# Two more gate pairs start their products ahead of the second half's norm, and TensorE multiplies a constant at the start

## The chip, the cores and the metric

One core of a Trainium2 chip runs the whole block. The metric is the device time of one execution in microseconds. In the names below PE is TensorE (the matrix engine), DVE is VectorE, ACT is ScalarE and SP is SyncE, whose queue issues nearly all DMAs. PEclk is the clock that TensorE was granted as a share of full speed: 1.00 is 2.4 GHz and 0.50 is 1.2 GHz.

## What is computed

One layer of an encoder block, in float32, on 16 meta tokens and 1024 positions of 1024 channels. Only the first part matters here:

```python
h = rmsnorm(h_res, g_mix_pre[l])
proj = h @ w_in[l]
u_a, c_g, b_g, v_b, gate_logits = jnp.split(proj, splits, axis=-1)

y_a = fourier_mix(u_a) @ w_fourier[l]

conv_in = c_g * v_b
y_b = (b_g * centred_dwconv(conv_in, conv_w_mix[l], conv_b_mix[l])) @ w_conv_out[l]

gates = jax.nn.sigmoid((gate_logits + b_gates[l]).reshape(bn, L, N_BRANCHES, D_MODEL))
merged = gates[:, :, 0] * y_a + gates[:, :, 1] * y_b
...
```

Behind it come the output projection, a second norm, a gated MLP with a depthwise convolution, and a last norm.

## The kernel before

**Numbers and products.** Activations lie with channels on partitions and positions along the row; two position halves of 514 columns each (`NH`) are worked on. A float32 operand is split into a high part (a rounding cast, L121, on ScalarE) and a low part (source minus high part, L122, on VectorE). A product is three matmuls per 128 channels: high by high (L153), low activation (L155), low weight (L157), each over two column parts of 258 and 256. `split` is the helper that records L121 and L122.

**Pairs.** Two blocks of 128 output channels and the two position halves are computed together by seven products instead of eight (Strassen-Winograd). `Pair.step` holds them. One product has 4 blocks of 128 channels, so 4 x 3 x 2 = 24 matmuls. Step 0 multiplies by the activation piece `b11` and step 4 by `b21`; both pieces come from the first position half alone. Steps 1, 2, 3, 5 and 6 use `t1`, `t2`, `t3`, `b22` and `t4`, which need the second half too. Step 5 adds to the PSUM tile `d` that step 1 began, and it may do so only when `g_s` (the sum of d and u, L138, in step 2) has read that tile.

**The first 100 us.** The kernel loads the positions' first half (`x1`) and the second (`x2`). One gate pair, (1,0), is computed naturally, without the pair scheme, in `natural`: for the first half while the loads come, with the norm applied to the result, and for the second half (natural(1)) while that half is normalised. Squares of the columns are summed on ScalarE and VectorE, a matmul with the constant `ones` makes the means (`ms_a`, `ms_b`, L433), and `rsqrt_of` makes the reciprocal root (r_a_y, r_a_t, r). `norm` (L438) scales by it on VectorE. Then VectorE makes low parts and the sums and differences of the two halves (L141).

Three gates are "early": `GATES[:NE1]` with `NE1 = 3`, that is (1,1), (1,2) and (1,3), which the trace names g_1, g_2 and g_3. Their weights for steps 0 and 4 are loaded and split by `early_pieces` (g_1e_0, g_1e_1 and so on), and the loop `for i in range(0, NE1, 2)` (L492) does those two steps, two gates at a time, before natural(1) begins in the code. The trace and the order name a gate by its last number only, so that g_0 and g_1 can also mean (0,0) and (0,1), and g_0 with nat the pair (1,0).

**Weights.** `Ring` has seven pieces (a high and a low tile each) and three raw buffers for loads. Four of the seven hold `wn`, the weights of the natural products, until natural(1) is done. Three circulate among the early gates until then.

**The jobs.** `run_pairs` (L320) then goes through 13 jobs: 7 gates and 6 pairs for the convolution branch (C, V, B twice). An early gate takes only steps `LATER` = (1, 2, 3, 5, 6); the others take all seven. While one job computes, the pieces of the next are made and the loads of the one behind that start. Hooks hang work for the Fourier branch on places (job, step): `transformed(kt)` (four matmuls on `wp`, L596, a load and a store) on step 3, and `fold(kt)` (vector work on a load, a store) on step 5 of jobs 3 to 10; `next_fold` loads the first folded blocks (`u`, L635) in the last job.

**What sets the order.** A scheduler places the instructions of each engine from the code's order and their dependences; `behind` and `issue_after` set lower bounds. What it made of the code is the order that each engine follows, and each engine runs its own list in order, SyncE's DMA queue included.

Of the kernel before, what the change touches and what calls it, by code (L numbers as in the profile page):

```python
# [17 lines left out]
P = 128  # L18
D = 1024
KT = D // P  # L20
# [61 lines left out]
def block_kernel(ctx, tc, xT, w_u, w_in, w_fa, w_fa2, w_fb, w_fb2, w_co, w_out, w_up, w_dn,  # L82
                 par, dch, cos_t, sin_t, outT):
    nc = tc.nc
# [21 lines left out]
    ones = const.tile([P, P], F32, name="ones")  # L106
# [3 lines left out]
    warm = const.tile([P, 1], F32, name="warm")  # L110
# [4 lines left out]
    def col(name, i=0, p=P):  # L115
        return pr[:p, _C[name] + i : _C[name] + i + 1]
# [20 lines left out]
    def add(out, a, b, eng=V):  # L137
        return eng.tensor_tensor(out=out, in0=a, in1=b, op=ALU.add).ins  # L138

    def sub(out, a, b, eng=V):  # L140
        eng.tensor_tensor(out=out, in0=a, in1=b, op=ALU.subtract)  # L141
# [124 lines left out]
    class Pair:  # L266


        us = 2
# [46 lines left out]
    def early_pieces(name, src, into=(None, None), eng=V):  # L316

        return ring.halves(f"{name}e", src, into, eng)
# [46 lines left out]
    ring.open(proj_s, "ring1", 7)  # L365
    gp = new_pool(keep_s, "gp", side="right")
    W1 = T0 + NH
    NE1 = 3
    GATES = [(1, 1), (1, 2), (1, 3), (0, 0), (0, 1), (0, 2), (0, 3)]

    class Gate(Pair):
        us = NE1 + 1

        def __init__(self, g, f):
            self.rows = (g * KT + f, g * KT + f + 4)
# [11 lines left out]
    with ExitStack() as st:  # L387
# [36 lines left out]
        def ms_tile(name):  # L424
            return psum.tile([P, 512], F32, tag="ms", name=name, bufs=2)

        ms_a = [ms_tile(f"ms1_a{i}") for i in range(2)]

        def half_norm(name, sums, n, out):
# [10 lines left out]
        def natural(half, kt, x, js=range(2)):  # L440
            for j in js:
                mm3(
                    subs(nat_out[half, j]),
                    tuple(a[:, kt % 4 * P : (kt % 4 + 1) * P] for a in wn[j][kt // 4]),
                    tuple([a[:, kt % 4, o : o + n] for o, n in SUB] for a in x),
                    kt == 0,
                    kt == KT - 1,
                )
# [12 lines left out]
        for kt in range(KT):  # L461
            if kt in (0, 3):
                for j in range(2):
                    i = kt // 3
# [4 lines left out]
                half_norm("a", next(sa), W1, r1[:, :W1])  # L469
            natural(0, kt, raw1[kt // 4])  # L470
        early = [Gate(*g) for g in GATES[:NE1]]
        ep = [early_pieces(p_.name, w_in[16 + p_.rows[0]]) for p_ in early]
        first = []

        def x_b(k):
            if k == 1:
                for j in range(2):
                    s = scratch["t3"][0][:, j, :]
                    mul(s, whole(nat_out[0, j]), r1[:, T0:W1])
                    first.append(s)  # L480
            norm(k, x1[k], r1[:, :W1])
            x1[k] = x1[k][:, T0:]
            put(hx["b11" if k < 4 else "b21"], k % 4, x1[k])
# [6 lines left out]
        for k in range(4, KT):  # L490
            x_b(k)
        for i in range(0, NE1, 2):  # L492
            for step, e in ((0, 0), (4, 1)):
                for p_, w in zip(early[i : i + 2], ep[i : i + 2]):
                    p_.step(psum, step, w[e], hx[PIECES[step]])
# [37 lines left out]
    class Conv(Pair):  # L533


        us = NE1 + 1

        def __init__(self, kind, j, state):
            self.kind, self.j, self.state = kind, j, state
# [40 lines left out]
    jobs = []  # L580
    for p_ in early + [Gate(g, f) for g, f in GATES[NE1:]]:
        jobs.append((p_, [w_in[16 + r] for r in p_.rows], LATER if p_ in early else ALL))
# [7 lines left out]
    def transformed(kt):  # L590

        r = ring.raw(f"wu{kt}")
        SP.dma_start(r[:, :512], w_u[kt])
        wp = wtile(psum, f"wp{kt}")[:, :512]
        for g in range(G):
            nc.tensor.matmul(wp[:, g * P : (g + 1) * P], r[:, g * P : (g + 1) * P], dc, start=True, stop=True)  # L596
        src = wp.rearrange("p (g k) -> p g k", k=P)
        t = r[:, 512:]
        for s, at, k in ((src[:, :, :KC], slice(0, NA), KC), (src[:, :, KC:], slice(NA, 512), KS)):
            S.copy(t[:, at].rearrange("p (g k) -> p g k", k=k), s)  # L600
        SP.dma_start(fold_d[kt, :, FW:], t)

    def fold(kt):

        t = pre.tile([P, 2 * H + HP], F32, tag="fold", name=f"fold{kt}", bufs=1)
        h, diff = t[:, : L + 1], t[:, 2 * H : 3 * H]
        SP.dma_start(h[:, :L], xT[:, kt, :])
        V.scalar_tensor_tensor(out=h[:, :L], in0=h[:, :L], scalar=col("g_pre", kt), in1=r1, op0=ALU.mult, op1=ALU.mult)
        V.tensor_copy(h[:, L : L + 1], h[:, 0:1])
        f0, rev = h[:, :H], h[:, L : L - H : -1]  # L610
        sub(diff, f0, rev)
        add(f0, f0, rev)
        c, s = t[:, H : 2 * H], t[:, :H]
        add(c[:, :Q], f0[:, :Q], f0[:, H - 1 : H - 1 - Q : -1])
        sub(c[:, Q:], f0[:, : Q - 1], f0[:, H - 1 : H - Q : -1])
        sub(s[:, :Q], diff[:, :Q], diff[:, H - 1 : H - 1 - Q : -1])
        add(s[:, Q:], diff[:, 1:Q], diff[:, H - 2 : H - 1 - Q : -1])
        SP.dma_start(fold_d[kt, :, :FW], t[:, :FW])
# [12 lines left out]
    def next_fold(kt):  # L631

        raw, hi, lo = (room(t, dt, f"u{kt}{i}") for i, (t, dt) in enumerate(zip(FOLD_ROOMS[kt], (F32, F32R, F32R))))
        w = FW + 512
        SP.dma_start(raw[:, :w], fold_d[kt])  # L635
        split(hi[:, :w], lo[:, :w], raw[:, :w])
        xs = [(hi[:, at : at + H], lo[:, at : at + H]) for at in (H, 0)]
        folded.append((xs, (hi[:, FW:w], lo[:, FW:w])))

    hooks = {(NE1 + kt, 3): lambda kt=kt: transformed(kt) for kt in range(KT)}  # L640
    for kt in range(KT):
        hooks[NE1 + kt, 5] = lambda kt=kt: fold(kt)
    hooks[len(jobs) - 1, 1] = lambda: next_fold(0)
    hooks[len(jobs) - 1, 2] = lambda: next_fold(1)
    hooks[len(jobs) - 1, 4] = lambda: next_fold(2)
# [64 lines left out]
    with ExitStack() as st:  # L710
# [18 lines left out]
        def table(tab, name, at):  # L729
            raw = room(at, F32, f"{name}r")[:LT, :TW]  # L730
            return raw, SP.dma_start(raw, tab).ins
# [7 lines left out]
        for kt in range(KT):  # L739
# [3 lines left out]
            if kt == 0:  # L743
                cos_r, _ = table(cos_t, "cos", "t4h")
# [143 lines left out]
    def load_merged(c):  # L888
        c0, n = CHM[c]
        v = valid(c)  # L890
        parts = []
        for k in range(0, KT, 3):
            e = min(k + 3, KT)
            t = ring.raw(f"mr{c}_{k}")[:, : (e - k) * n].rearrange("p (k n) -> p k n", n=n)
            SP.dma_start(t[:, :, :v], merged_d[:, k:e, c0 + TM - T0 : c0 + TM - T0 + v])
            if v < n:
                V.memset(t[:, :, v:], 0.0)
            parts += [merged_parts(c, kt, t[:, kt - k])[0] for kt in range(k, e)]
        merged[c] = parts
# [32 lines left out]
    def norm_a(c):  # L932
        c0, n = CHM[c]
        v = valid(c)
        ms = next(z[c])
        rr = np_.tile([P, W], F32, tag="rr", name=f"rr{c}", bufs=2)[:, :n]
        got = rsqrt_of(f"r2_{c}", scratch, ms, n, rr)
        sq = squares(f"h{c}", n)
        next(sq)
        xr = []  # L940
        for f in range(0, KT, 2):
            t = eo.tile([P, 2 * W], F32, tag="o", name=f"xr{c}_{f}", bufs=4)
            t = t.rearrange("p (f n) -> p f n", f=2)
            SP.dma_start(t[:, :, :v], xT[:, f : f + 2, TM + c0 : TM + c0 + v])
            xr += [t[:, i, :v] for i in range(2)]
        for f in range(KT):
            h = h_at(c, f)
            scaled = mul(h, h, rr).ins
            add(h[:, :v], h[:, :v], xr[f])
            sq.send(h)  # L950
            SP.dma_start(hres_d[:, f, c0 : c0 + v], h[:, :v])
        z[c] = sq
        return got, scaled
# [8 lines left out]
    def norm_b(c):  # L962
        c0, n = CHM[c]
        if c not in rs:
            inverse(c)
        rr = rs[c]
        A, B = second(c)
        for f in range(KT):
            h = h_at(c, f)
            V.scalar_tensor_tensor(out=h, in0=h, scalar=col("g_fpre", f), in1=rr, op0=ALU.mult, op1=ALU.mult)  # L970
            if c < 2:
                a, e = max(c0, 1), min(c0 + n, NH + 1)
                put(hx["b11" if f < 4 else "b21"], f % 4, hA[f // 4][:, f % 4, a:e], a - 1, e - a)
            elif f < 4:
                sub(A(f), h, A(f))
                put(hx["t1"], f, A(f), c0 - 513, n)
            else:
                put(hx["b22"], f - 4, B(f), c0 - 513, n)
# [16 lines left out]
    def mean_b(c):  # L995
        z[c] = next(z[c])
# [118 lines left out]
    ep = [None]  # L1115
# [18 lines left out]
    for c in range(1, 4):  # L1134
        hooks = {0: lambda: norm_a(c - 1), 5: lambda: (load_merged(c + 1), mean_b(c - 1), norm_b(c - 1))}
        order = range(KT)
        if c == 3:
            order = (6, 7, 0, 1, 4, 5, 2, 3)
            hooks = {
                0: lambda: norm_a(2),  # L1140
                3: lambda: plain.load(0, "t1h"),
                4: lambda: first_blocks("t3h"),
                5: lambda: (mean_b(2), inverse(2)),
            }
# [7 lines left out]
    early = lambda step, i: ups[i].step(psum, step, ep[i][step // 4], hx["b11" if step == 0 else "b21"])  # L1152
# [309 lines left out]
```

## Time and profile before

| | us |
|---|---|
| median of three runs | 1236.94 |
| the three runs | 1235.50, 1236.94, 1240.91 |
| the profiled execution | 1235.98 |
| its span, first to last instruction | 1234.2 |
| PE busy in the span | 1182.5 |
| DVE busy | 1004.5 |
| ACT busy | 549.3 |
| mean granted clock of PE | 0.985 |

Times within the trace are counted from the span's start. A busy time is what an engine's instructions took; a wait is the idle time ahead of an instruction, with the instruction that ended it. Matmuls overlap, so the distance from one start to the next tells their pace better than their duration does. Where several instructions of one form follow each other, a row of a timeline joins them, with their number as x2, x4 and so on.

### The profile page before, as it was taken

How to read it: one execution, taken by the hardware profiler on the slowest of the kernel's cores; microseconds unless marked ns; L12 is line 12 of the kernel's file. 1: busy time of each engine (PE TensorE's matmuls, PEld its weight loads, DVE VectorE, ACT ScalarE, POOL GpSimd, SP SyncE). 2: the span in 40 equal slices, each digit the busy share in tenths (PEclk: the TensorE clock that was granted, in tenths of full speed). 3: DMA queues.
4: the chain of work that ended last, by engine and by line, in shares of the span. 5: the costliest groups of instructions: out<-in, count | busy, mean ns of one | idle time of the engine just before them, and what ended most of it. 6: DMA issues, size and time to landing. Idle time of an engine off the chain costs nothing.

```text
span 1234.2 us, 22254 instructions
## 1 busy us (share of the span) xinstructions
PE 1182.5 (96%) x8800; PEld 1136.5 (92%) x8800; DVE 1004.5 (81%) x1771; ACT 549.3 (45%) x997; POOL 0.4 (0%) x6
## 2 busy tenths in 40 slices
PE   7979999999999899999989999999999999999995
PEld 6879999999998899898989999999999998888884
DVE  8998757766677766889999988899888989866678
ACT  6733433322352235655644435443444444454562
POOL 0000000000000000000000000000000000000000
PEclk8989999999999999999989999999999999999998
DMA  6245554221786755562233332232223289344433
GB/s 245 87 129 191 173 188 157 98 99 50 252 244 205 242 184 104 133 109 86 86 112 112 112 112 69 95 129 95 89 84 120 96 313 327 127 158 124 130 126 137
DMA packets 75016, 176.65 MB, mean 143 GB/s; under 512 B 7550, under 2 KB 24526, under 8 KB 74912
## 3 DMA queue, kind: packets, MB, share of 16 engines
q1 hardware_dynamic: 74768, 175.11, 44.7%
q8 instruction: 69, 1.13, 0.4%
q14 instruction: 35, 0.29, 0.1%
q10 hardware_dynamic: 144, 0.12, 0.0%
HBM read 126.57 MB, written 48.63 MB: 142 GB/s over the span
## 4 chain that ended last, share of the span: by engine, by line
PE 76%; DVE 14%; DMA 7%; ACT 2%; issue 1%; DVEq 0%; SPq 0%; ACTq 0%
DMA wor<-in_w_out_dram 3%; PE up_d L153 3%; PE up_d L155 3%; PE up_d L157 3%; PE up_a L153 3%; PE up_a L157 3%; PE up_c L157 3%; PE up_c L155 3%; PE up_c L153 3%; PE up_a L155 3%; PE dna L155 3%; PE dna L153 3%; PE dna L157 3%; PE dnb L155 2%; PE dnb L153 2%; PE dnb L157 2%
## 5 line engine op out<-in xcount | busy, mean ns | idle before, releaser
L153 PE MATMUL mo<-mh,wo 128*128 128x258 f32 (+1 forms) x256 | 73.4, 287 | 0.0
L157 PE MATMUL mo<-mh,wo 128*128 128x258 f32 (+1 forms) x256 | 72.4, 283 | 0.0
L155 PE MATMUL mo<-ml,wo 128*128 128x258 f32 (+1 forms) x256 | 72.2, 282 | 0.0
L153 PEld LDWEIGHTS mo<-mh,wo 128*128 128x128 f32 x256 | 48.5, 189 | 0.4 <-ACT hA L926 0.2
L155 PEld LDWEIGHTS mo<-ml,wo 128*128 128x128 f32 x256 | 48.5, 189 | 0.2
L157 PEld LDWEIGHTS mo<-mh,wo 128*128 128x128 f32 x256 | 48.5, 189 | 0.0
L1077 ACT ACTIVATE up_1o<-up_1x,pr 128x512 f32<-128x512 f32 x33 | 27.0, 817 | 42.4 <-DVE up_1x L138 42.4
L1081 ACT ACTIVATE up_0o<-up_0o 128x512 f32<-128x512 f32 x44 | 27.8, 632 | 31.9 <-DVE up_0o L1079 31.7
L121 ACT CAST up_1h<-up_1t 128x512 fp32r<-128x512 f32 x11 | 6.8, 620 | 78.0 <-DVE up_1t L138 78.0
L153 PE MATMUL up_d<-b22h,up_5h 128*128 128x258 f32 (+1 forms) x168 | 34.8, 290 | 6.3 <-DVE up_0x L138 6.1
L138 DVE TENSOR_TENSOR up_u<-up_b,up_u 128x514 f32<-128x514 f32 x21 | 14.6, 695 | 29.0 <-PE up_b L157 28.9
L155 PE MATMUL up_d<-b22l,up_5h 128*128 128x258 f32 (+1 forms) x168 | 34.8, 290 | 0.0
L157 PE MATMUL up_d<-b22h,up_5l 128*128 128x258 f32 (+1 forms) x168 | 34.5, 287 | 0.0
L157 PE MATMUL up_c<-t3h,up_3l 128*128 128x258 f32 (+1 forms) x168 | 33.9, 283 | 0.4 <-DVE up_3l L122 0.4
L157 PE MATMUL up_d<-t1h,up_1l 128*128 128x258 f32 (+1 forms) x168 | 33.6, 281 | 0.5 <-DVE up_1l L122 0.5
L153 PE MATMUL up_d<-t1h,up_1h 128*128 128x258 f32 (+1 forms) x168 | 33.9, 282 | 0.1
L153 PE MATMUL up_b<-t2h,up_2h 128*128 128x258 f32 (+1 forms) x168 | 33.9, 283 | 0.0
L153 PE MATMUL up_c<-t3h,up_3h 128*128 128x258 f32 (+1 forms) x168 | 33.8, 283 | 0.0
L157 PE MATMUL up_c<-t4h,up_6l 128*128 128x258 f32 (+1 forms) x168 | 33.8, 282 | 0.0
L155 PE MATMUL up_c<-t3l,up_3h 128*128 128x258 f32 (+1 forms) x168 | 33.7, 281 | 0.0
L155 PE MATMUL up_c<-t4l,up_6h 128*128 128x258 f32 (+1 forms) x168 | 33.7, 282 | 0.0
L157 PE MATMUL up_b<-t2h,up_2l 128*128 128x258 f32 (+1 forms) x168 | 33.7, 282 | 0.0
(1298 smaller groups left out, 4344.9 us busy)
## 6 DMA issues: line engine op xcount, KB each, us to landing
g<-gp_d SPq DMA_DIRECT2D x35, 512.0 KB
up_1r<-in_w_up_dram SPq DMA_DIRECT2D x22, 512.0 KB
gp_d<-up_0o SPq DMA_DIRECT2D x44, 256.0 KB
up_0r<-in_w_up_dram SPq DMA_DIRECT2D x20, 512.0 KB
s<-sig_d SPq DMA_DIRECT2D x16, 514.0 KB
sig_d<-g_s SPq DMA_DIRECT2D x30, 257.0 KB
u<-fold_d SPq DMA_DIRECT2D x8, 777.0 KB
fold_d<-fold SPq DMA_DIRECT2D x8, 521.0 KB
```

Source lines behind the costliest of these rows:

```text
L121: a = copy(hi, src)
L138: return eng.tensor_tensor(out=out, in0=a, in1=b, op=ALU.add).ins
L153: nc.tensor.matmul(o, wh, h, start=first, stop=False, **kw)
L155: nc.tensor.matmul(o, wh, l, start=False, stop=False, **kw)
L157: newest[:] = [nc.tensor.matmul(o, wl, h, start=False, stop=last, **kw).ins]
L1077: S.activation(t, ap[:, 1 : 1 + HALF], AF.Identity, bias=col("cb_ffn", b), scale=w(1))
L1081: S.activation(t, t, AF.Gelu_apprx_tanh)
```

## The change

The constant `NE1` goes from 3 to 5, so that (0,0) and (0,1) are early too: their steps 0 and 4 come before the jobs, and their jobs keep five steps. The number of `u` tiles, `NE1 + 1` = 4 before, is `NE1` = 5 now. The weights of the first three early gates are loaded where all were; the others' are asked for within the loop. Eleven matmuls of the constant `ones` by itself stand ahead of everything on TensorE, into a PSUM tile of the `ms` kind that is not read. The hooks hang on jobs `NE1 + kt` and so move from jobs 3 to 10 to jobs 5 to 12; the last fold hangs on step 0, since step 5 of the last job has a hook of its own.

```diff
-    NE1 = 3
+    NE1 = 5
...
     class Gate(Pair):
-        us = NE1 + 1
+        us = NE1
...
+        w0 = ms_tile("warm")[:, :P]
+        for _ in range(11):
+            nc.tensor.matmul(w0, ones, ones, start=True, stop=True)
         ms_a = [ms_tile(f"ms1_a{i}") for i in range(2)]
...
         early = [Gate(*g) for g in GATES[:NE1]]
-        ep = [early_pieces(p_.name, w_in[16 + p_.rows[0]]) for p_ in early]
+        first_weights = lambda ps: [early_pieces(p_.name, w_in[16 + p_.rows[0]]) for p_ in ps]
+        ep = first_weights(early[:3])
...
         for i in range(0, NE1, 2):
+            ep += first_weights(early[len(ep) : i + 2])
             for step, e in ((0, 0), (4, 1)):
                 for p_, w in zip(early[i : i + 2], ep[i : i + 2]):
                     p_.step(psum, step, w[e], hx[PIECES[step]])
...
     class Conv(Pair):
-        us = NE1 + 1
+        us = NE1
...
     hooks = {(NE1 + kt, 3): lambda kt=kt: transformed(kt) for kt in range(KT)}
     for kt in range(KT):
-        hooks[NE1 + kt, 5] = lambda kt=kt: fold(kt)
+        hooks[NE1 + kt, 5 if kt < KT - 1 else 0] = lambda kt=kt: fold(kt)
```

How this moves instructions is shown on three engines. First VectorE, where the norm of the second half begins (x_2_118 and its like are columns of the second half, t4 holds high and low parts of it, t3l and x_2_110 are the first half's columns). Before:

```order
L122 TENSOR_TENSOR t4l<-x_1_117,t4h 128x514
L141 TENSOR_TENSOR t3l<-x_1_117,t3l 128x514
L438 SCALAR_TENSOR_TENSOR x_2_118<-x_2_118,pr,r_83 128x514
L438 SCALAR_TENSOR_TENSOR x_3_119<-x_3_119,pr,r_83 128x514
L141 TENSOR_TENSOR x_2_110<-x_2_118,x_2_110 128x514
L122 TENSOR_TENSOR t4l<-x_2_118,t4h 128x514
L122 TENSOR_TENSOR t4l<-x_3_119,t4h 128x514
```

The same place in VectorE's list now:

```order
L122 TENSOR_TENSOR g_0e_0l<-g_0er,g_0e_0h 128x512
L141 TENSOR_TENSOR t3l<-x_1_117,t3l 128x514
L122 TENSOR_TENSOR g_0e_1l<-g_0er,g_0e_1h 128x512
L442 SCALAR_TENSOR_TENSOR x_2_118<-x_2_118,pr,r_83 128x514
L442 SCALAR_TENSOR_TENSOR x_3_119<-x_3_119,pr,r_83 128x514
L141 TENSOR_TENSOR x_2_110<-x_2_118,x_2_110 128x514
L122 TENSOR_TENSOR t4l<-x_2_118,t4h 128x514
L122 TENSOR_TENSOR g_1e_0l<-g_1er,g_1e_0h 128x512
L122 TENSOR_TENSOR t4l<-x_3_119,t4h 128x514
L141 TENSOR_TENSOR x_3_111<-x_3_119,x_3_111 128x514
L442 SCALAR_TENSOR_TENSOR x_4_120<-x_4_120,pr,r_83 128x514
L122 TENSOR_TENSOR g_1e_1l<-g_1er,g_1e_1h 128x512
```

Four low parts of weights (g_0e_0l, g_0e_1l, g_1e_0l, g_1e_1l) stand among the columns of the second half. Second, ScalarE at the same place, before:

```order
L384 ACTIVATE g_1_s_482<-g_1_a,pr 128x514
L384 ACTIVATE g_2_s_509<-g_2_a,pr 128x514
L121 CAST t1h<-t3l 128x514
L284 COPY g_3_u<-g_3_a 128x514
L121 CAST t1h<-t3l 128x514
L121 CAST t4h<-x_2_118 128x514
L121 CAST t4h<-x_3_119 128x514
```

And now:

```order
L384 ACTIVATE g_1_s_494<-g_1_a,pr 128x514
L121 CAST g_0e_0h<-g_0er 128x512
L384 ACTIVATE g_2_s_521<-g_2_a,pr 128x514
L121 CAST g_0e_1h<-g_0er 128x512
L284 COPY g_3_u<-g_3_a 128x514
L121 CAST t1h<-t3l 128x514 x2
L121 CAST t4h<-x_2_118 128x514
L121 CAST g_1e_0h<-g_1er 128x512
L284 COPY g_0_u<-g_0_a 128x514
L121 CAST t4h<-x_3_119 128x514
```

The casts of the new pieces stand between sigmoids of earlier gates and casts of t4. Third, TensorE behind step 0 of g_3, before:

```order
L157 MATMUL g_3_a<-b11h,g_3e_0l 128x256
L153 MATMUL nat_0_566<-t4h,wn_0h 128x258
L153 MATMUL nat_0_566<-t4h,wn_0h 128x256
L155 MATMUL nat_0_566<-t4l,wn_0h 128x258
L155 MATMUL nat_0_566<-t4l,wn_0h 128x256
L157 MATMUL nat_0_566<-t4h,wn_0l 128x258
L157 MATMUL nat_0_566<-t4h,wn_0l 128x256
L153 MATMUL g_3_a<-b21h,g_3e_1h 128x258
```

And now:

```order
L157 MATMUL g_3_a<-b11h,g_3e_0l 128x256
L153 MATMUL g_0_a<-b11h,g_0e_0h 128x258
L153 MATMUL g_0_a<-b11h,g_0e_0h 128x256
L155 MATMUL g_0_a<-b11l,g_0e_0h 128x258
L155 MATMUL g_0_a<-b11l,g_0e_0h 128x256
L157 MATMUL g_0_a<-b11h,g_0e_0l 128x258
L157 MATMUL g_0_a<-b11h,g_0e_0l 128x256
```

Step 0 of g_0 follows step 0 of g_3, then come step 4 of both and step 0 of the second g_1; natural(1) begins behind that, and step 4 of this g_1 stands behind its first six matmuls.

## Rows read from the trace of the kernel before

**Rows 1.** Busy time by stretch: PE, PEld, DVE, ACT, POOL; PEclk; DMA share.

```profile
core 0: us, PE busy (x) PEld busy (x) DVE busy (x) ACT busy (x) POOL busy (x), PEclk, DMA share, GB/s
...
45.00:59.80 14.80, 14.80 (x122) 14.49 (x121) 14.80 (x25) 9.44 (x17) 0.00 (x0) 1.00 0.28 89
59.80:62.70 2.90, 0.13 (x2) 0.04 (x1) 2.90 (x6) 2.90 (x7) 0.00 (x0) 1.00 0.48 182
62.70:74.10 11.40, 9.63 (x71) 8.82 (x72) 11.40 (x20) 4.58 (x8) 0.00 (x0) 1.00 0.31 98
74.10:78.10 4.00, 0.30 (x4) 0.12 (x2) 3.98 (x10) 0.62 (x1) 0.00 (x0) 0.66 0.46 133
78.10:82.10 4.00, 4.00 (x19) 4.00 (x20) 4.00 (x8) 1.34 (x2) 0.00 (x0) 0.50 0.17 66
82.10:88.00 5.90, 5.90 (x50) 5.90 (x50) 5.32 (x12) 3.69 (x6) 0.00 (x0) 0.99 0.25 64
```

**Rows 2.** Waits of PE, 0 to 330 us: us in total, times, longest.

```profile
PE nat L153 <- DVE wn_0h L121: 6.4, 1, 6.4
PE g_d L153 <- DVE g_s L138: 3.7, 1, 3.7
PE g_d L153 <- ACT g_1h L121: 2.8, 1, 2.8
...
PE g_a L153 <- ACT g_3e_0h L121: 0.5, 1, 0.5
```

**Rows 3.** Chain of waits, ahead of step 5: start, us, what.

```profile
74.20 1.91 DVE t4l L122 x4
...
77.26 0.70 DVE g_s L138
```

**Rows 4.** Timeline of PE: steps 5 and 6 of job 0; steps 0 and 1 of job 12.

```profile
78.09 0.77 PE L153 MATMUL g_d<-b22h,g_5h 128*128 128x258 f32 x2 [3.70 <-DVE g_s L138]
...
82.85 0.41 PE L153 MATMUL g_c<-t4h,g_6h 128*128 128x258 f32 x2
...
302.66 0.40 PE L153 MATMUL B_a<-b11h,B_0h 128*128 128x258 f32 x2
...
305.54 0.41 PE L153 MATMUL B_d<-t1h,B_1h 128*128 128x258 f32 x2
```

**Rows 5.** Timeline of DVE: a weight's low part and the row behind it.

```profile
43.53 0.69 DVE L122 TENSOR_TENSOR g_3e_1l<-g_3er,g_3e_1h 128x512 fp32r<-128x512 f32 x1
44.14 0.69 DVE L122 TENSOR_TENSOR t4l<-x,t4h 128x514 fp32r<-128x514 f32 x1
```

**Rows 6.** Waits of ACT, 15 to 80 us: those of weight casts.

```profile
ACT g_3e_0h L121 <- ACT g_2e_1h L121: 1.0, 1, 1.0
...
ACT g_3e_1h L121 <- PE g_a L155: 0.6, 1, 0.6
```

**Rows 7.** Chain of waits, 100 to 140 us: products of wp.

```profile
126.11 0.89 PE wp L596 x8
```

**Rows 8.** Chain of waits: first, ninth and tenth pair of nat's matmuls.

```profile
6.35 0.77 PE nat L153 x2
...
10.14 0.43 PE nat L157 x2
10.57 0.26 PE nat L153 x2
```

**Rows 9.** Timeline of DVE where the first half's mean comes back.

```profile
19.10 0.70 DVE L138 TENSOR_TENSOR sq_b<-sq_b,b22l 128x514 f32<-128x514 f32 x1
19.90 0.43 DVE L163 SCALAR_TENSOR_TENSOR r_a_t<-r_a_y 128x263 f32<-128x263 f32 x1
```

**Rows 10.** Chain of waits in the last job of the projection.

```profile
305.73 4.30 DMA u<-fold_d
```

**Rows 11.** Waits of PE, 280 to 480 us: the one for u.

```profile
PE pq L724 <- DVE u L122: 0.4, 1, 0.4
```

**Rows 12.** Timeline of ACT: the cast of a weight piece.

```profile
42.88 0.62 ACT L121 CAST g_3e_1h<-g_3er 128x512 fp32r<-128x512 f32 x1 [0.62 <-PE g_a L155]
```

## The prediction

> **What bounds the kernel now.** I read the profile in four steps: busy time by stretch for the first 90 us, then TensorE's waits, then the chain of waits, then single instructions. The whole-kernel figures (PE busy 96% of the span) hide the place of the change, so the reader should look at stretches. From 45.0 to 78.1 us VectorE is idle for 0.02 us in all [rows 1]. TensorE in the same time is busy 14.80 of 14.80, then 0.13 of 2.90, then 9.63 of 11.40, then 0.30 of 4.00 us [rows 1]. So until 78 us VectorE makes the pace: it makes the normalised second half, its sums and all the low parts, and TensorE runs out of products. Two waits of TensorE show where, 2.8 us for the first weights of job 0 and 3.7 us for the sum g_s that frees the tile of step 5 [rows 2]. The chain of waits runs along VectorE's queue through this stretch; its last pieces are the four low parts of t4, then g_u and g_s, and then step 5 [rows 3]. From 82.1 us on TensorE is the bound: it is busy all of 5.90 us [rows 1], and the view of its waits up to 330 us names none later than step 5's. From there on, a product less is time less.
>
> **The pause costs twice.** Step 5 of job 0 has its first matmuls at 78.09 us and step 6 follows at 82.85, so it takes 4.76 us. A product step of 24 matmuls in the same kernel, from 302.66 to 305.54 us, takes 2.88 us, which is 0.12 us per matmul [rows 4]. The granted clock explains it: 0.66 while TensorE paused, 0.50 (the 1.2 GHz level) over 78.1 to 82.1 us, 0.99 behind [rows 1].
>
> **What is moved.** Gates (0,0) and (0,1) now do steps 0 and 4 in the starved stretch and no longer in jobs 3 and 4. These are 4 products of 24 matmuls: 4 x 2.88 = **-11.5 us** behind 83 us, where nothing else hides or replaces them.
>
> In the starved stretch they must fit. Before, the 120 matmuls from the natural product at 45.07 us on (96 of natural(1), 24 of g_3's step 4) take 14.4 us. With 96 more and the 72 of job 0's steps 1 to 3 it is 288 x 0.12 = 34.6 us, so step 3 ends at 79.6 us if TensorE never waits.
>
> VectorE gets four more instructions, the low parts g_0e_0l, g_0e_1l, g_1e_0l, g_1e_1l, all ahead of g_s. One of the same form, g_3e_1l, started at 43.53 us and the row behind it at 44.14 [rows 5]: 0.6 us each, 4 x 0.6 = 2.4 us. With a queue that has no gap, that is **+2.4 us** on the start of step 5: 78.1 becomes 80.5. TensorE, ready at 79.6, has 0.9 us to spare. The high parts, two copies and two sigmoids go to ScalarE, which is busy 9.44 of 14.80 us there [rows 1]; they cost nothing as long as none waits.
>
> **The clock.** With TensorE working from 45 to 80 us with hardly a gap, step 5 should run as at 302 us: 4.76 - 2.88 = **-1.9 us**. Its bounds are 0 (a pause before step 5 lasts as long as before) and -1.9. I take the whole, since the two gaps of 2.8 and 3.7 us shrink to one below 1 us.
>
> **The waits that are new.** Three weight pieces circulate as long as natural(1) holds the other four, so each new high part waits on ScalarE until a product has released a slot, and the t4 and b22 casts queue behind it. Rows of this kind exist: the cast of g_3e_0h stood 1.0 us (put down to ScalarE's own cast, which was done long before, so it was something else; I take it for the slot) and that of g_3e_1h 0.6 us behind a product [rows 6]. ScalarE lags, VectorE may then wait for a high part, and TensorE for a low one. Bounds: 0, if ScalarE's slack takes it, and 4 x 1.0 = 4 us, if each of four waits reaches the end. TensorE's 0.9 us takes the first of it, and VectorE can lose time only where its next row waits. I take **+0.5 us**, nearest to the lone 0.5 us by which TensorE waited for such a piece [rows 2].
>
> **The constant products.** Eleven 128-column matmuls come ahead of the first natural product. Those of the same form on wp stand eight in 0.89 us, two records for a product (so 0.22 us for one) [rows 7], which makes 2.4 us at full clock and 4.9 us at half. They read only the constant, so they fit into the 6.4 us that TensorE waits at the start [rows 2]. Today nat's pairs of matmuls stand 0.43 us apart from 6.35 to 10.57 us (nine of them, at the 1.2 GHz level by that spacing), and then 0.26 [rows 8]; a running clock from the start would end them some 9 x 0.19 = 1.7 us earlier. But who waits for that? The next that needs TensorE is r_a_t on VectorE, by way of the mean and ScalarE. VectorE, which is in order, does sq_b from 19.10 us for 0.70, and r_a_t starts at 19.90 [rows 9]. So only 0.1 us can be won at the place where VectorE takes over: **-0.1 us**. The bounds are 0 and, if those waits all shrink with TensorE, -1.7.
>
> On this the Trainium skill ("TensorE: Matmul & The Clock Gate", Part 1, What's actually happening) says that the throttled state is the default and that activity releases it. The rows of nat agree with it; by that rule alone the constant products would be worth the whole 1.7 us and the result would be 1.6 us lower than mine, were TensorE what is waited for.
>
> **What else is moved.** The extra loads of two weights come earlier in SyncE's queue, at DMA shares of 0.28 to 0.48 [rows 1]: nothing. The hooks of the fold and of wp go two jobs later, so that the last two wp products (2 x 0.89 us) stand in other jobs, with the same total. The order puts one store of wu (256 KB) among the u loads of the last job. A u load of 777 KB took 4.30 us from 305.73 on [rows 10], so this store is worth 1.4 us of queue by size, while TensorE waits only 0.4 us for u [rows 11]. I take 0; the bounds are 0 and 4.3 us, a whole load's delay.
>
> **Sum.** -11.5 + 2.4 - 1.9 + 0.5 - 0.1 = -10.6 us, against the profiled execution's 1235.98 us: 1225.4. The median of the runs shown is 0.96 us above that execution, so on its base I predict **1226.3 us**, -0.9%.
>
> **Rivals.** *Partial gain.* TensorE is now as full as VectorE, with 0.9 us to spare, so each further wait in 45 to 80 us is paid. Four waits of 1.0 us instead of my 0.5 in all make +3.5: 1229.8; and if step 5 then starts cold again, 1231.7. For it speak rows 6, against it that ScalarE has a third of its time free. 13%.
>
> *Given back at the end of the projection.* The chain from 305.73 us on runs through u loads, ScalarE, VectorE and more loads [rows 10], not through TensorE. If it does not move up with job 12, up to 4.3 us come back in TensorE's waits: 1230.6. For it speaks the wu store in front of a u load; against it that the u load starts when the b11 tile is free, which job 12 itself decides. 8%.
>
> *The constant pays in full.* 1.6 us lower, 1224.7. 6%.
>
> *Slower: the ring locks.* ScalarE and VectorE are in order, so a high part that waits for a slot holds up the t4 or b22 cast behind it, natural(1) starts later, and natural(1) is what frees the four other slots. Each of the four new pieces then costs a product (2.88), its cast (0.62 [rows 12]) and its low part (0.60) one after the other, 4.1 us, and TensorE idles meanwhile. It decides against the change as soon as the holds exceed 11.5 + 1.9 = 13.4 us: four full ones are 16.4 us, +3.0, 1239.9; for more than 0.5% a fifth hold, on a t4 or b22 cast, would have to come (20.5 us, +7.1, 1244.0). Against it: in the order the early pieces stand between rows that are ready, and three pieces are enough for one product at work and one in preparation. 4%, half of it past the 0.5%.
>
> The Trainium skill ("TensorE: Matmul & The Clock Gate", the table at its head) calls ScalarE's and VectorE's queues strictly first in, first out. The g_3e rows agree, and this is what would turn a late piece into a lock.
>
> *The constant does not warm anything.* The first nat pairs stay 0.43 us apart; time as forecast, +0.1. It is part of the main case.
>
> **Numbers.** Forecast 69% (1224.8 to 1228), partial gain 13%, given back 8%, constant in full 6%, lock 4%. Below 1222.5 I see no term; at the top 1231.5 holds the partial gain and the return at the end. About 0.5%, 6.2 us, is what a measurement of this kernel tells from no change. Faster by more means below 1230.8: forecast, constant, most of the two partial cases, 0.86. Within it: the tail of those cases and half of the lock, 0.12. Slower: 0.02.
>
> **What would show it.** Right: the first nat pairs 0.24 us apart, yet r_a_t within 0.2 us of 19.90; no gap of 2.8 us at 60 and none of 3.7 us before step 5; step 5 of job 0 near 80.5 to 81 us at clock 1.00 and 2.9 us long; jobs 3 and 4 with five products each; the first pq matmul about 10.5 us earlier than now; VectorE without gaps in 45 to 80 us. Wrong: waits of ScalarE for a ring piece that show up on VectorE and TensorE, step 5 past 83 us, or a first wait for u of several us at the end of the projection.

## The result and the profile after

The changed kernel takes 1230.15 us in the median of six runs (1224.68 to 1231.73), the kernel before 1238.48 us in the median of six. The ratio is 0.9926 with a 95% interval of 0.9908 to 0.9944, so it is faster by 0.7%, some 9 us. The forecast was 1226.3 us with a range of 1222.5 to 1231.5; on the base that it used, 1236.94 us, it asked for 10.6 us less, and the interval of the ratio reaches from 7 to 11 us. The profiled execution of the changed kernel took 1231.41 us with a span of 1229.6 us; it is one of its slower ones, and that of the kernel before was one of its faster ones, so that the two traces lie only 4.6 us apart at their ends. I compare them stage by stage.

Busy time by stretch in the changed kernel, with the columns of [rows 1]:

```profile
45.00:59.80 14.80, 14.80 (x123) 14.63 (x122) 14.80 (x25) 11.51 (x22) 0.00 (x0) 1.00 0.55 174
59.80:62.70 2.90, 2.90 (x27) 2.90 (x26) 2.90 (x6) 2.23 (x5) 0.00 (x0) 1.00 0.22 82
62.70:74.10 11.40, 11.40 (x97) 11.40 (x96) 11.40 (x20) 6.45 (x12) 0.00 (x0) 1.00 0.28 92
74.10:80.00 5.90, 5.81 (x49) 5.60 (x47) 5.88 (x12) 1.83 (x3) 0.00 (x0) 1.00 0.64 198
...
311.70:313.90 2.20, 0.04 (x1) 0.00 (x0) 2.17 (x3) 0.56 (x1) 0.00 (x0) 1.00 0.89 360
313.90:317.20 3.30, 3.26 (x15) 3.29 (x16) 2.40 (x2) 0.93 (x1) 0.00 (x0) 0.51 0.88 270
```

The first four rows answer to [rows 1]: where TensorE was busy 0.13 of 2.90 and 9.63 of 11.40 us, it is now busy all the time, and VectorE is still full. The last two rows are new. Behind the last product of the projection TensorE stands still for 2.2 us, and then its clock is at 0.51 for 3.3 us. The waits of TensorE from 0 to 340 us (us in total, times, longest) say for what:

```profile
PE pq L730 <- DVE B_s L138: 2.2, 1, 2.2
...
PE nat L153 <- DVE wn_0h L121: 0.3, 1, 0.3
PE g_d L153 <- DVE g_s L138: 0.3, 1, 0.3
```

Of [rows 2], the wait for g_s went from 3.7 to 0.3 us and the one for job 0's first weights (2.8 us) is not there any more. A third one is gone too, which the rows ahead of the prediction leave out (before, the same view):

```profile
PE g_c L155 <- DVE t3l L122: 1.8, 3, 1.3
```

In their place stands a wait of pq, the first product of the Fourier stage, for VectorE's B_s; pq waited 0.4 us for u before [rows 11]. The timeline of TensorE has the places that answer to [rows 4], then pq and the first matmul of the Fourier transforms' second stage (the tiles dft):

```profile
80.24 0.50 PE L153 MATMUL g_d<-b22h,g_5h 128*128 128x258 f32 x2 [0.33 <-DVE g_s L138]
...
83.22 0.40 PE L153 MATMUL g_c<-t4h,g_6h 128*128 128x258 f32 x2
...
302.88 0.37 PE L153 MATMUL B_a<-b21h,B_4h 128*128 128x258 f32 x1
...
313.94 0.51 PE L730 MATMUL pq<-u 128*105 128x260 f32 x1 [2.20 <-DVE B_s L138]
...
344.22 0.28 PE L153 MATMUL dft<-cosh,pqh 105*87 105x262 f32 x1
```

Step 5 starts at 80.24 us and step 6 at 83.22, so step 5 takes 2.98 us where it took 4.76. In the kernel before, the last two of these places are here, with the first dft behind them:

```profile
314.15 0.40 PE L153 MATMUL B_a<-b21h,B_4h 128*128 128x258 f32 x2
...
322.76 0.28 PE L724 MATMUL pq<-u 128*105 128x260 f32 x1
...
352.20 0.28 PE L153 MATMUL dft<-cosh,pqh 105*87 105x262 f32 x1
```

Step 4 of the last job comes 11.27 us earlier than before, and pq only 8.82 us. With the slow clock behind pq, the second stage (dft) starts at 344.22 in place of 352.20 us, 7.98 us earlier. So the change won 11.3 us and gave 3.3 us of it back within 45 us of the trace. What VectorE does there is this, in its timeline of the changed kernel:

```profile
311.42 1.78 DVE L122 TENSOR_TENSOR u<-u,u 128x1554 fp32r<-128x1554 f32 x1 [1.09 <-ACT u L121]
313.11 0.69 DVE L138 TENSOR_TENSOR B_s<-B_c,B_u 128x514 f32<-128x514 f32 x1
```

B_s reads the PSUM tile of step 6 (B_c). It stands in VectorE's queue behind a low part of u, which waited 1.09 us for ScalarE. That pq must wait for this add at all was not so before: there pq started at 322.76 us, and the same add only behind it:

```profile
323.96 0.69 DVE L138 TENSOR_TENSOR B_s<-B_c,B_u 128x514 f32<-128x514 f32 x1
```

### The profile page after: what moved, and what is told of

Read it like the earlier page. It is cut to its first block, busy times and chain, and to the rows that moved or that the text cites. A ratio compares the mean times of both kernels' runs of the same rounds, so it can differ in the third digit from the quotient of the medians.

```text
span 1229.6 us, 22306 instructions
## 1 busy us (share of the span) xinstructions
PE 1187.5 (97%) x8822; PEld 1141.5 (93%) x8822; DVE 1004.6 (82%) x1771; ACT 548.9 (45%) x997; POOL 0.4 (0%) x6
## 4 chain that ended last, share of the span: by engine, by line
PE 76%; DVE 14%; DMA 5%; ACT 2%; issue 2%; DVEq 0%; SPq 0%; ACTq 0%
DMA wor<-in_w_out_dram 3%; PE up_a L153 3%; PE up_a L157 3%; PE up_d L153 3%; PE up_a L155 3%; PE up_d L157 3%; PE up_d L155 3%; PE up_c L157 3%; PE up_c L155 3%; PE up_c L153 3%; PE dna L153 3%; PE dna L155 3%; PE dna L157 3%; PE pq L730 2%; PE dnb L155 2%; PE dnb L157 2%
## 5 line engine op out<-in xcount | busy, mean ns | idle before, releaser
L153 PE MATMUL mo<-mh,wo 128*128 128x258 f32 (+1 forms) x256 | 74.9, 293 | 0.0
L157 PE MATMUL mo<-mh,wo 128*128 128x258 f32 (+1 forms) x256 | 73.5, 287 | 0.0
L153 PEld LDWEIGHTS mo<-mh,wo 128*128 128x128 f32 x256 | 49.9, 195 | 0.5 <-ACT hA L932 0.2
L157 PEld LDWEIGHTS mo<-mh,wo 128*128 128x128 f32 x256 | 49.8, 194 | 0.0
```

Source lines behind the costliest of these rows:

```text
L153: nc.tensor.matmul(o, wh, h, start=first, stop=False, **kw)
L157: newest[:] = [nc.tensor.matmul(o, wl, h, start=False, stop=last, **kw).ins]
```

## The experiments

**Two theories** for the wait of pq. *Bank*: the kernel sums its products in PSUM tiles, which the program places in numbered banks. The Fourier stage's first tile takes over a bank from the projection's tiles, of which four rotate. An early gate gets its first tile elsewhere, so with two more early gates two tiles fewer are drawn, the rotation ends two places further, and the bank is now that of step 6, which VectorE reads last. *Transfer*: the store of wu, which now stands among the loads of u in SyncE's queue, holds the chain of u. The first three runs tell them apart. The table gives medians, ratios to the kernel before in the same rounds with their intervals, and three distances (in us) out of the timeline of each profiled execution: from the first early product (g_a) to step 6 of job 0, from there to pq, and from there to the first dft.

| kernel | median us | ratio | g_a to step 6 | step 6 to pq | step 6 to dft |
|---|---|---|---|---|---|
| before | 1238.48 | | 54.84 | 239.91 | 269.35 |
| changed | 1230.15 | 0.9926 (0.9908 to 0.9944) | 55.37 | 230.72 | 261.00 |
| e1_bank_moved | 1228.88 | 0.9925 (0.9907 to 0.9944) | 56.20 | 228.34 | 258.15 |
| e2_bank_alone | 1239.62 | 1.0007 (0.9993 to 1.0022) | 55.36 | 242.04 | 272.33 |
| e3_wp_early | 1231.15 | 0.9942 (0.9924 to 0.9961) | 55.35 | 230.57 | 260.85 |
| e4_no_constant | 1229.15 | 0.9929 (0.9910 to 0.9947) | 55.35 | 231.19 | 261.47 |
| e5_low_twice | 1233.21 | 0.9965 (0.9950 to 0.9979) | 57.96 | 230.92 | 261.21 |
| e6_four_early | 1235.44 | 0.9976 (0.9962 to 0.9989) | 55.89 | 234.15 | 265.12 |
| e7_constant_alone | 1238.42 | 1.0009 (0.9995 to 1.0022) | 55.44 | 239.89 | 269.82 |
| e8_joined | 1229.27 | 0.9931 (0.9910 to 0.9952) | 56.32 | 228.28 | 257.12 |
| e9_changed_again | 1229.32 | 0.9925 (0.9905 to 0.9945) | 55.37 | 231.10 | 262.54 |
| e10_joined_again | 1229.72 | 0.9929 (0.9906 to 0.9952) | 56.17 | 228.28 | 258.46 |
| e11_bank_by_act | 1228.27 | 0.9923 (0.9905 to 0.9941) | 55.36 | 228.28 | 257.02 |
| e12_bank_by_act_store | 1228.97 | 0.9921 (0.9903 to 0.9939) | 55.37 | 228.26 | 257.21 |

### The bank, turned in the changed kernel: e1_bank_moved

```diff
     psum = new_pool(proj_s, "psum1", 4, space=PSUM)
+    for _ in range(3):
+        nc.tensor.matmul(wtile(psum, "skip")[:, :P], ones, ones, start=True, stop=True)
```

> The changed kernel with three more small products of the constant (0.22 us each) into PSUM tiles of the projection's pool, ahead of job 0. They turn the rotation of the four tiles by three, so that the first tile of the Fourier stage (pq) takes a bank that wp had, and no longer the one that the last sum B_s reads. Theory bank: the wait of pq on VectorE (2.2 us) and the half clock behind it go; the Fourier stage starts some 2.2 us earlier and the whole is 2 to 3 us shorter than the changed kernel, less 0.7 us for the products, so about 1.0% under the kernel before. Theory transfer (the store of wu in front of a load of u holds the chain of u): the wait stays, now for u, and the whole is 0 to 1 us longer than the changed kernel.

The wait for B_s is gone, and a smaller one for u stands in its place (waits of TensorE, 290 to 345 us):

```profile
PE pq L732 <- DVE u L122: 0.8, 1, 0.8
```

From step 6 on, pq comes 2.4 us and dft 2.85 us sooner than in the changed kernel. The bank was what pq waited for. The products themselves cost 0.8 us ahead of step 6 (56.20 against 55.37). Less the products, 1.3 to 2.3 us were expected. By the medians, which come from different rounds, the gain over the changed kernel is 1.3 us; by the ratios (0.9925 against 0.9926) it is 0.1 us, and the forecast of about 1.0% under the kernel before lies just outside its interval. So the trace shows that the wait goes, and the times do not show a gain.

### The bank alone, in the kernel before: e2_bank_alone

```diff
     psum = new_pool(proj_s, "psum1", 4, space=PSUM)
+    for _ in range(1):
+        nc.tensor.matmul(wtile(psum, "skip")[:, :P], ones, ones, start=True, stop=True)
```

> The kernel before with one small product of the constant into a tile of the projection's PSUM pool ahead of job 0 and nothing else: three early gates, the hooks where they were. The rotation now gives pq the bank that the last sum B_s reads. Theory bank: a wait of pq on VectorE of 1.5 to 2.5 us appears with a slow clock behind it, and the whole is 2 to 3.5 us (0.2 to 0.3%) longer than before. Theory transfer: no wait, +0.2 us.

One small product, with three early gates and everything else as before, makes the wait appear:

```profile
326.26 0.44 PE L726 MATMUL pq<-u 128*105 128x260 f32 x1 [1.98 <-DVE B_s L138]
326.50 0.64 PE L726 MATMUL pq<-u,u 128*105 128x260 f32 x2
326.93 0.41 PE L726 MATMUL pq<-u 128*105 128x252 f32 x1
```

The first three matmuls take 0.67 us here (326.26 to 326.93), about twice what they take at full clock (0.36 us in e12). With the wait and the slow clock, dft comes 2.98 us later behind step 6; 2 to 3.5 us were expected of the whole. The whole is +0.9 us by the ratio, with an interval from -0.9 to +2.7: the trace shows the mechanism, the end time does not resolve it.

The addresses in the built programs say the same. The first pq tile lies in the bank of B_c in all six kernels whose pq waits for B_s (the changed kernel, e2, e3, e4, e5 and e9) and in none of the other eight.

### The transfer: e3_wp_early

```diff
-    hooks = {(NE1 + kt, 3): lambda kt=kt: transformed(kt) for kt in range(KT)}
+    hooks = {(NE1 - 2 + kt, 3): lambda kt=kt: transformed(kt) for kt in range(KT)}
```

> The changed kernel with the products of wp, their loads and stores back on jobs 3 to 10, so that no store of wu stands among the loads of u; the banks rotate as in the changed kernel (pq still takes the bank that B_s reads). Theory bank: the wait of pq on VectorE's B_s stays at 1 to 2.5 us and the time is within 1.5 us of the changed kernel. Theory transfer: the wait goes, and the time is 2 to 3 us under the changed kernel.

No store of wu stands among the loads of u here, and the wait is as it was:

```profile
PE pq L730 <- DVE B_s L138: 2.1, 1, 2.1
```

The distances from step 6 are those of the changed kernel (230.57 and 260.85). Theory transfer falls; e12 shows it from the other side. The move of the folds by two jobs and the fifth u tile were not run by themselves.

### The constant: e4_no_constant and e7_constant_alone

```diff
-        w0 = ms_tile("warm")[:, :P]
-        for _ in range(11):
-            nc.tensor.matmul(w0, ones, ones, start=True, stop=True)
```

> The changed kernel without the eleven products of the constant. My forecast: TensorE is not what is waited for in the first 20 us; nat starts at half clock, r_a_t starts within 0.2 us of the changed kernel's, and the time is 0 to 0.3 us longer than the changed kernel's. Rival: the running clock counts in full, and without it the time is 1.6 to 2 us longer.

e7_constant_alone has these lines added to the kernel before, and nothing else.

> The kernel before with the eleven products of the constant and nothing else. My forecast: the first pairs of nat stand 0.24 us apart in place of 0.43, r_a_t on VectorE starts within 0.2 us of 19.9 by the load's spread, time within 0.5 us of before. Rival: 1.6 to 2 us shorter.

The first matmuls of nat, from the timelines of e4 and then e7:

```profile
6.20 0.77 PE L153 MATMUL nat<-t1h,wn_0h 128*128 128x258 f32 x2 [6.20 <-DVE wn_0h L121]
6.76 0.63 PE L155 MATMUL nat<-t1l,wn_0h 128*128 128x258 f32 x2
7.20 0.64 PE L157 MATMUL nat<-t1h,wn_0l 128*128 128x258 f32 x2
```

```profile
6.24 0.48 PE L153 MATMUL nat<-t1h,wn_0h 128*128 128x258 f32 x2 [0.74 <-DVE wn_0h L121]
6.55 0.41 PE L155 MATMUL nat<-t1l,wn_0h 128*128 128x258 f32 x2
6.80 0.41 PE L153 MATMUL nat<-t1h,wn_0h 128*128 128x258 f32 x2
```

By this spacing TensorE runs at its faster rate with the constant and at little more than half of it without: pairs stand 0.25 and 0.44 us apart. The granted clock does not show it; PEclk reads 1.00 from 6.0 to 10.2 us in both traces. VectorE's r_a_t, in the changed kernel and then in e4:

```profile
19.75 0.43 DVE L163 SCALAR_TENSOR_TENSOR r_a_t<-r_a_y 128x263 f32<-128x263 f32 x1
```

```profile
20.31 0.43 DVE L163 SCALAR_TENSOR_TENSOR r_a_t<-r_a_y 128x263 f32<-128x263 f32 x1 [0.48 <-ACT r_a_y L162]
```

Without the constant r_a_t comes 0.56 us later, and VectorE stands still for it for 0.48 us; within 0.2 us was expected of e4, so this part of its forecast failed. In e7 r_a_t starts at 19.96 us, against 19.90 before [rows 9], but the add sq_b ahead of it started later too (19.36 against 19.10). From that add's start to r_a_t's it is 0.60 or 0.61 us in eight of the nine profiled executions with the constant (1.06 in e1), and 0.72 to 1.17 in the five without. So something like 0.1 to 0.6 us is won at this place. The first early product starts at 27.16 to 29.05 us in the nine (middle one 28.06) and at 28.01 to 28.95 in the five (28.77), a spread in which such a gain cannot be read off. The times do not show it either: without the constant 0.9929, with it 0.9926; alone 1.0009 (0.9995 to 1.0022). A gain of 1.6 to 2 us is ruled out.

### VectorE's chain: e5_low_twice

```diff
-            return [self.piece(f"{name}_{i}", r[:, i * 512 : (i + 1) * 512], into=into[i], eng=eng) for i in range(2)]
+            ps = [self.piece(f"{name}_{i}", r[:, i * 512 : (i + 1) * 512], into=into[i], eng=eng) for i in range(2)]
+            for i, (hi, lo) in enumerate(ps if name in TWICE else ()):
+                sub(lo, r[:, i * 512 : (i + 1) * 512], hi.bitcast(F32))
+            return ps
```

(`TWICE` holds the names of the two new gates' weights.)

> The changed kernel with the low parts of the two new gates' weights computed twice on VectorE (four more instructions of 0.6 us ahead of g_s; the second result is the same as the first). Theory VectorE (its queue sets when step 5 of job 0 starts): step 5 starts 2.4 us later than in the changed kernel, near 82.6 us, TensorE's wait for g_s grows from 0.3 to 2.7 us, and step 5 may run at half clock again: 2.4 to 4.3 us longer in all. Theory TensorE (it is the bound up to 80 us): step 5 within 0.5 us of the changed kernel and the time within 1 us.

```profile
83.43 0.48 PE L153 MATMUL g_d<-b22h,g_5h 128*128 128x258 f32 x2 [2.23 <-DVE g_s L138]
...
86.36 0.40 PE L153 MATMUL g_c<-t4h,g_6h 128*128 128x258 f32 x2
```

Step 5 starts 3.19 us later than in the changed kernel, of which 0.55 us is a later start of the early products (28.40 against 27.85); 2.64 us is left for four instructions, 0.66 us each. So VectorE's queue does set step 5, and the price of a low part was right. The clock stayed at full rate behind the 2.2 us pause (step 5 took 2.93 us), so in the trace the smaller of the two expected costs came: g_a to step 6 is 2.6 us longer. The time is longer by 3.1 us by the medians of different rounds and by 4.8 us by the ratios (0.9965 against 0.9926), each with an interval of some 2 us, so the times do not tell the two costs apart.

### Half of the move: e6_four_early

```diff
-    NE1 = 5
+    NE1 = 4
...
-    hooks = {(NE1 + kt, 3): lambda kt=kt: transformed(kt) for kt in range(KT)}
+    hooks = {(4 + kt, 3): lambda kt=kt: transformed(kt) for kt in range(KT)}
...
-        hooks[NE1 + kt, 5 if kt < KT - 1 else 0] = lambda kt=kt: fold(kt)
+        hooks[5 + kt, 5 if kt < KT - 1 else 0] = lambda kt=kt: fold(kt)
```

> The changed kernel with four early gates in place of five: two products moved and two low parts added, the products of wp on jobs 4 to 11 and the folds as in the changed kernel; the banks rotate so that pq takes the one of step 5. Theory of the sum: VectorE's chain is 1.2 us longer (step 5 near 79.3 us), TensorE is through with step 3 near 74 and still pauses for some 5 us in all, so step 5 runs at half clock and takes 4.8 us: -5.8 + 1.2 = -4.6 us against the kernel before (0.996). Rival (the clock and the gap close in proportion): step 5 takes 3.8 us, -5.5 us. If TensorE's pauses are gone already: -6.5 us.

```profile
79.40 0.59 PE L153 MATMUL g_d<-b22h,g_5h 128*128 128x258 f32 x2 [3.70 <-DVE g_s L138]
...
83.86 0.40 PE L153 MATMUL g_c<-t4h,g_6h 128*128 128x258 f32 x2
```

Step 5 starts at 79.40 us (79.3 expected) and takes 4.46 us (4.8), so with one gate more the first pause goes, and the second stays whole, with most of the slow clock's cost behind it (the rival expected 3.8 us). From step 6 to pq it is 5.76 us less than before, two products to the hundredth. Up to pq the sum is 4.75 us won, of 4.6 expected; then 1.5 us of waits for u follow (waits of TensorE, 290 to 360 us):

```profile
PE pq L730 <- DVE u L122: 1.5, 2, 1.0
```

The kernel before had 0.4 us of them. Why u comes late here and not in e12 is not shown. At dft 3.2 us are left, and the ratio, 0.9976, says 3.0 us with an interval from 1.4 to 4.7.

### A version without the wait: e8, e10, e11 and e12

e8_joined takes the constant out, puts wp on jobs 3 to 10 and has the three small products of e1; e10 is the same kernel again, in the same rounds as e9, the changed kernel again.

> What the runs point to, joined: five early gates without the eleven products at the start, wp back on jobs 3 to 10 (no store of wu among the loads of u), and three small products of the constant ahead of job 0 that turn the PSUM rotation so that pq's first bank is the one of step 4's sum. Bank theory with the store's small share: no wait of pq, some 3 us under the changed kernel less 0.7 for the products, so 1227 to 1228.5 by the median, 0.991 to 0.992 of before. If the wait of pq comes from anything else it stays and the time is that of the changed kernel.

> The changed kernel as it is, on the same chip and in the same rounds as the joined kernel, since their difference (3.9 us at the start of the Fourier transforms by the traces, 0.9 us by the medians of different rounds) is smaller than what one set of rounds tells. Both theories: 1228 to 1231 us, 0.992 to 0.994 of before.

> The joined kernel again (five early gates, no products of the constant at the start, wp on jobs 3 to 10, the PSUM rotation turned by three). If what the bank wait costs reaches the end: 2.5 to 4 us under the changed kernel of the same rounds. Rival: the stages behind the Fourier transforms take it back (their waits are for VectorE and for loads): within 1 us of the changed kernel.

The wait for B_s is gone in both (e10 has one of 1.2 us for u), and dft comes 257.12 and 258.46 us behind step 6, against 261.00 and 262.54 in the changed kernel. But the medians of e9 and e10 are 1229.32 and 1229.72: the 2.5 to 4 us that e10 should have won if the wait reached the end are not there, and its rival, within 1 us of the changed kernel, came true. e8 missed its 1227 to 1228.5 us as well (1229.27). One price that this version pays is in its traces: its small products take 0.8 to 0.95 us ahead of step 6. Its early products also start later, at 28.95 and 28.77 us against 27.85 and 27.90, but only 0.1 to 0.3 us of that lie between sq_b and r_a_t, where the constant counts; the rest is there before. So e11 keeps the constant, has wp on jobs 3 to 10 and turns the rotation with ScalarE instead, and e12 does that with wp where the change has it:

```diff
     psum = new_pool(proj_s, "psum1", 4, space=PSUM)
+    for _ in range(3):
+        S.copy(wtile(psum, "skip")[:, :1], eps_t)
```

> The changed kernel with the constant products at the start kept, wp on jobs 3 to 10, and the PSUM rotation turned by three with three one-column copies on ScalarE in place of the three products on TensorE, which had cost 0.9 us by the traces. Bank theory: step 6 of job 0 starts as in the changed kernel (83.2 us by an equal start), pq does not wait for B_s, the Fourier transforms start 3 to 4 us earlier than in the changed kernel, and if nothing behind takes it back the time is 1226 to 1227 us, 0.990 to 0.991 of before. Rival (the stages behind absorb it): 0.9925 as for the changed kernel.

> The same with wp on jobs 5 to 12 as in the changed kernel, so that the store of wu stands among the loads of u. Bank theory: no wait for B_s; a wait for u below 1 us may show in its place, so 0 to 1 us longer than the one without the store. Transfer theory: the wait of pq stays at 2 us or more.

The timeline of TensorE in e12 at the end of the projection, and then VectorE's add there:

```profile
310.55 0.40 PE L157 MATMUL B_c<-t4h,B_6l 128*128 128x258 f32 x2
310.79 0.28 PE L732 MATMUL pq<-u 128*105 128x260 f32 x1
310.90 0.41 PE L732 MATMUL pq<-u,u 128*105 128x260 f32 x2
```

```profile
312.06 0.69 DVE L138 TENSOR_TENSOR B_s<-B_c,B_u 128x514 f32<-128x514 f32 x1
```

pq follows the last product without a gap, 1.3 us ahead of the add for which it waited in the changed kernel. The store of wu stands among the loads of u in e12, and pq waits for nothing: no cost of that store is seen here. Both versions start dft 3.8 to 5.5 us sooner behind step 6 than the two profiles of the changed kernel, at 340.61 and 339.74 us against 344.22 and 345.81.

In the end times little of this is seen: 0.9923 and 0.9921 against 0.9926 and 0.9925, with intervals of 0.0018 to 0.0020 on each side, and medians of different rounds of 1228.27 and 1228.97 against 1230.15 and 1229.32 us. Their ratios are the lowest of all, by 0.2 to 0.6 us, and that difference is not shown. e11 was expected at 1226 to 1227 us and 0.990 to 0.991; it came nearer to its rival, 0.9925, though its interval reaches both.

Among the kernels with five early gates, from dft to the last matmul the five executions with the wait took 868.7 to 873.4 us (mean 870.9) and the five without it 870.2 to 873.0 (mean 871.9). The stretch splits at the first matmul of the output projection (the tiles mo). Up to there those with the wait took 92.7 to 94.3 us (mean 93.3) and those without it 93.6 to 96.7 (mean 95.0); behind it the means are 777.6 and 776.9. So some 1.6 of the 4 us may be taken back between dft and mo, and that is argued from ten executions, not tested; where the rest goes stays open.

## Why the prediction was right, and what was wrong in it

**The moved products (-11.5).** Right. From step 6 to pq the kernels with two more early gates and no wait for B_s take 228.26 to 228.34 us, the kernel before 239.91: 11.6 us less. e6 has exactly half.

**VectorE's four low parts (+2.4).** Right, and tested. From the first early product to step 5 it was 50.08 us before and is 52.39 now, +2.3; e6 with two more of them than before has +1.35, e5 with eight more +4.95.

**The clock of step 5 (-1.9).** Right: 4.76 became 2.98 us, -1.8. e6, where step 5 still takes 4.46 us, shows that most of it comes only with the second gate.

**The waits for pieces (+0.5).** Too high: there is no sign of them on TensorE. The holds exist on ScalarE in the changed kernel (waits of ScalarE, 15 to 85 us), and they are of the size of [rows 6]:

```profile
ACT g_1e_1h L121 <- PE g_a L155: 0.7, 1, 0.7
...
ACT g_3e_1h L121 <- PE g_a L155: 0.6, 1, 0.6
```

But VectorE had work that was ready, and TensorE was never held: the 0.3 us for g_s is all that it waited in 45 to 90 us. So the lock, the slower rival, and the partial gain both fell.

**The constant (-0.1).** Right in that it is small, and somewhat too small where it was priced. The text took the time that VectorE stands still ahead of r_a_t, 0.1 us by [rows 9]. From sq_b's start to r_a_t's it was 0.80 us there and is 0.61 now, so 0.2, and in e4 0.6. The Trainium skill ("TensorE: Matmul & The Clock Gate", Part 1, What's actually happening) says that activity releases the throttle; the spacing agrees, with pairs at 0.25 us in place of 0.44. The 1.7 us that would follow from it alone are not in the times of e4 and e7.

**The end of the projection (0, bounds 0 and 4.3).** This is the step that failed. The text priced what the change put into SyncE's queue there and took 0, and it gave a loss of up to 4.3 us 8% as a rival, with the store of wu in front of a load of u as its cause. The loss came, 3.3 us at dft, but from elsewhere: the text did not ask where the next stage's tiles lie. Two gates that draw their first tile elsewhere are also two tiles less in a rotation of four, and pq's first bank changed hands. Its term should have been the wait of 2.2 us and a clock at 0.51 over the 3.3 us behind it.

The sum up to dft, by terms as measured: +0.4 at step 6, -11.6 for the products, +2.4 for the wait of pq, +0.8 from pq to dft (30.28 against 29.44 us, of which the kernel before spent 0.4 waiting for u), which makes -8.0 us, as the two traces have it. The ratio says -9.2 with an interval from -11.4 to -6.9. What lies behind dft differs by up to 4.7 us among the fourteen profiled executions, whichever kernel it is, as much as the two profiled executions lie apart at their ends.

That the time came out inside the range owes something to luck. The median, 1230.15 us, lies above the 1224.8 to 1228 us of the main case; it is inside the range because the range's top had been set for losses, and the loss that came had another cause than those priced. The kernel before adds to it: its median was 1238.48 us beside the changed kernel, 1.5 us over the base that the forecast stands on. On that base the ratio gives 1227.8 us, just inside the main case, where the two traces at dft leave 2.6 us less than the -10.6 of the sum.

## What to carry to other kernels

Work that needs only the first half of a norm can fill the pause in which another engine prepares the second half; its price is what it adds to that engine's queue, and here 11.6 us of products cost 2.3 us there. A filled pause pays a second time only when it is filled far enough that the clock does not fall: with one gate more step 5 still took 4.46 us, with two it took 2.98. When a change alters how many tiles a pool hands out, look at which bank the next stage's first tile inherits, and who reads that bank last; one tile more turned a wait of 2 us on in the kernel before (e2), and three more turned it off in the changed one (e1).

## What was not expected of the hardware

Pauses of about the same length had different sequels. In e5 TensorE paused 2.2 us ahead of step 5 and its clock read 1.00 behind; in the changed kernel it paused 2.2 us ahead of pq and the clock read 0.51 for the next 3.3 us. The stretches, with the columns of [rows 1], of e5 and then of e6, whose pause was 3.7 us:

```profile
81.20:83.40 2.20, 0.00 (x0) 0.00 (x1) 2.18 (x7) 0.00 (x0) 0.00 (x0) 1.00 0.50 202
83.40:86.40 3.00, 2.97 (x25) 3.00 (x26) 3.00 (x6) 1.35 (x2) 0.00 (x0) 1.00 0.07 29
```

```profile
75.70:79.40 3.70, 0.00 (x1) 0.03 (x1) 3.68 (x9) 0.46 (x1) 0.00 (x0) 1.00 0.49 144
79.40:83.10 3.70, 3.70 (x18) 3.70 (x19) 3.70 (x7) 1.35 (x2) 0.00 (x0) 0.54 0.19 71
```

In the kernel before, the pause of 2.8 us near 60 us was followed by 1.00 as well [rows 1]. So a pause of about 2 us can cost its own length, or 1.3 to 1.5 us more: from pq to dft the changed kernel takes 30.28 us, and e8, e11 and e12, where TensorE does not wait in that stretch, 28.74 to 28.95. Why it goes one way or the other is not shown here.
